# The displaced low part of every eighth k: 192 bytes instead of 160

## The chip, the cores and the metric

The kernel runs on one core of one Trainium2 chip. A core has a matrix engine (TensorE, PE in the profile, with its weight loads as PEld), VectorE (DVE), ScalarE (ACT), GpSimd (POOL) and SyncE (SP), which here issues most of the DMAs. They share an on-chip memory of 128 partitions (SBUF); TensorE writes its sums to a second one (PSUM). The metric is the device time of one execution in microseconds (us), the median of several.

## The reference

The reference is one layer of a decoder over 256 positions with 2048 channels, in float32. Cut to what matters here, it is a row of matrix products with small work between them:

```python
h = rms_norm(x, ln1[l])
proj = h @ w_in[l]                       # GDN q|k|v, beta, decay, gate z; MoBA q|k|v; gates A, B
y_a = gated_deltanet(qkv_a, beta_a, decay_a, z_a, ...) @ w_branch_a[l]
y_b = moba_attention(q_b, k_b, v_b) @ w_branch_b[l]
merged = jax.nn.sigmoid(gate_a) * y_a + jax.nn.sigmoid(gate_b) * y_b
x = x + merged @ w_out[l]
h = rms_norm(x, ln2[l])
u = causal_dwconv(h @ w_up[l], ffn_conv[l], ffn_conv_bias[l])
u_gate, u_val = jnp.split(u, 2, axis=-1)
x = x + (jax.nn.silu(u_gate) * u_val) @ w_down[l]
return rms_norm(x, final_norm)
```

## The kernel before

**Products in two parts.** Every large product is computed from float32 operands that are split in two: a high part in the type `float32r`, and a low part, what is left (`split` and `low`, lines 116 to 121: ACT casts, DVE subtracts). Three matmuls then stand for one: high weight with high operand, high weight with low operand, low weight with high operand. The weights come by DMA in pieces of 1 MB (`fetch`, issued by SP), are split into the tiles `wh` and `wl` (`load_w`), and are the stationary operand, 128 columns at a time. The activations, transposed, are the moving (streamed) operand, 256 columns of 4 bytes, so 1024 bytes in each partition.

**Where the activations lie.** `Parts` (line 152) holds such a split operand in one flat tile. `kt` is the number of 128-row slices of the inner dimension: 16 for 2048 rows, 8 for 1024. For each k the high part lies first and the low part behind it, 1024 bytes each. Eight k make a group (`GROUP`), and each group has 64 elements of room behind it, so that group follows group at 4160 elements. `at(k, a)` gives the place of part `a` (0 high, 1 low) of slice k. In each group the low part of the last k alone (k = 7 and 15) is pushed on by `TURN` elements, into that room; the high parts and all other low parts are not. `one` is a view of one part, `two` of the same part of two neighbouring k. `two` takes the step between the two from `at`, so that it follows the displacement.

Five operands are kept so: `hc` (the first normalized input, 16 k), `yca` and `ycb` (the branches' outputs, 8 k each), `mc` (the merged branches, 16 k) and `h2` (the second normalized input, 16 k, `h` in the profile, in the place of `hc`). They are written by `scaled` (lines 210 and 211) or by `split` and `low`.

**Where the weights lie.** `wh` and `wl` are tiles of 2048 + 64 elements in two buffers each. `chunk` places the weights in them 24 elements (96 bytes) from the start, except for the stages named in `PLACE`: 8 elements for `ps_v`, 16 for `ps_wo`. `load_w` for the last product (`w_dn`) uses the start itself. Weight block follows weight block at 512 bytes.

**The order of the matmuls.** `block` (line 188) runs over k and for each k over the three products: `wh` with the high part, `wh` with the low part, `wl` with the high part. All go through `main_mm` (line 109, its matmul is line 110). `chunk` (line 195) makes two such blocks into one PSUM tile. The stages follow each other as the program is written: `ps_gdn` and `ps_z` (GDN projections; the first two blocks of all use float32 matmuls at line 255 on the raw input), `ps_bd` (line 299: the 16 columns of beta and decay, with the weights `wb2` of 48 columns for each k, its two products through `mmg`), `ps_moba` and `ps_v`, `ps_gate` (16 chunks), `ps_br` (8 chunks for each branch, in turn), `ps_wo` (8 chunks; the first of them in four pieces), `ps_up` (44 chunks), and `pd` (the last product, 512 streamed columns, whose streamed operand is the weights; `Parts` has no share in it). In `ps_v` the operand `hc` is the stationary one.

Beside this stream runs the small work of the two branches (`bg`): `main_mm` counts an estimate of the time that it has issued, and at each 1700 ns lets the generators `gdn`, `moba`, `decay` and `rotary` issue their next piece (`tick`). Their matmuls stand between those of the stages up to the middle of `ps_gate`; behind that nothing of them is left. At the start of `ps_up` two groups of matmuls for the row sums (`rstd`, tile `R`, line 98) stand in the stream, one ahead of it and one within its first block.

Of the kernel before, what the change touches and what calls it, by code (L numbers as in the profile page):

```python
# [27 lines left out]
EPS = 1e-6  # L28
EVERY = 1700
PLACE = {"v": 8, "wo": 16}  # L30
TURN = 40
GROUP = 8
ATT_SCALE = 128 ** -0.5
CONST_FIELDS = [
# [48 lines left out]
def layer_kernel(ctx: ExitStack, tc: tile.TileContext, xT, pos, cst, csel, ceye, vec, convw, ffw, bdv,  # L83
# [68 lines left out]
    class Parts:  # L152
# [6 lines left out]
        def at(self, k, a):  # L159
            return k // GROUP * self.size + (2 * (k % GROUP) + a) * T + TURN * (a and k % GROUP == GROUP - 1)  # L160

# [748 lines left out]
```

## Time and profile before

| | |
|---|---|
| time, median of 3 runs | 1507.69 us (1507.61 to 1507.84) |
| the profiled execution | 1512.56 us |
| its span, first to last instruction | 1510.8 us |
| mean granted TensorE clock | 0.995 |
| TensorE matmuls busy | 1494.0 us, 11471 of them |
| TensorE weight loads busy | 1434.1 us |
| VectorE, ScalarE, GpSimd busy | 968.2, 721.1, 121.1 us |
| HBM read | 271.68 MB, 182 GB/s over the span |

Matmuls are pipelined, and the busy time of a matmul is longer than its distance to the next one, so a share of 99% says that TensorE is never empty, not that it is at its fastest. What counts is the distance from the start of one matmul to the start of the next, and this is read from the timeline. There each row has its start and its length in us, the engine, the line, what it writes and reads, and how many like it in a row are merged (x2). In the page's chain of waits the shares are those of the span.

### The profile page before, as it was taken

The page shows a single profiled execution, that of the slowest core. Times are in us where ns is not written, and L with a number is a line of the kernel's source. Part 1 is how long each engine was busy: PE and PEld are TensorE (multiplying, and loading weights), DVE is VectorE, ACT ScalarE, POOL GpSimd, SP SyncE. Part 2 cuts the span into 40 slices and gives each one's busy share as a digit, 9 for nine tenths or more (in the row PEclk, how much of TensorE's full clock was granted, in tenths as well). Part 3 has the DMA queues.
Part 4 walks back from the last instruction along what each step waited for, and adds up shares of the span by engine and source line. Part 5 has one row for each costly group of instructions (what it writes and reads, how often), then busy time and mean ns, then how long its engine had stood idle before and what let it go on. Part 6 is the DMA issues. An engine that isn't in the chain of part 4 may idle for free.

```text
span 1510.8 us, 26931 instructions
## 1 busy us (share of the span) xinstructions
PE 1494.0 (99%) x11471; PEld 1434.1 (95%) x11471; DVE 968.2 (64%) x1373; ACT 721.1 (48%) x948; POOL 121.1 (8%) x133
## 2 busy tenths in 40 slices
PE   9999999999999999999999999999999999999998
PEld 8999999998999999999999999999999998888886
DVE  7988695886665445666666666666666665555554
ACT  5655363434474433445455444454444554444444
POOL 0001011042120000110100000000000000000000
PEclk9999999999999999999999999999999999999999
DMA  9445444444336553568555555555555554555552
GB/s 341 171 148 184 171 153 162 152 158 144 136 126 209 195 182 125 183 215 303 195 171 195 193 195 187 183 189 196 195 184 184 192 195 167 195 196 195 195 195 84
DMA packets 45657, 277.23 MB, mean 184 GB/s; under 512 B 5504, under 2 KB 6992, under 8 KB 15456
## 3 DMA queue, kind: packets, MB, share of 16 engines
q1 hardware_dynamic: 43712, 270.98, 52.0%
q0 software_dynamic: 960, 2.36, 0.5%
q10 hardware_dynamic: 864, 2.16, 0.4%
q8 instruction: 90, 1.47, 0.4%
q14 instruction: 31, 0.25, 0.0%
HBM read 271.68 MB, written 3.80 MB: 182 GB/s over the span
## 4 chain that ended last, share of the span: by engine, by line
PE 90%; DVE 5%; ACT 2%; DMA 1%; issue 1%; SPq 0%; DVEq 0%; POOLq 0%; ACTq 0%
PE ps_up L110 32%; PE pd L98 16%; PE ps_gate L110 11%; PE ps_gdn L110 8%; PE ps_wo L110 6%; PE ps_br L110 5%; PE ps_moba L110 3%; PE ps_z L110 3%; PE ps_v L110 2%; DVE wl L117 2%; ACT wh L120 1%; DMA wraw<-in_w_gdn 1%; PE g L98 1%; PE py L552 0%; PE pu L558 0%
## 5 line engine op out<-in xcount | busy, mean ns | idle before, releaser
L117 DVE TENSOR_TENSOR wl<-wraw,wh 128x1024 fp32r<-128x1024 f32 (+1 forms) x500 | 607.1, 1248 | 221.6 <-ACT wh L120 221.0
L120 ACT CAST wh<-wraw 128x1024 fp32r<-128x1024 f32 (+1 forms) x500 | 497.5, 1040 | 481.2 <-PE ps_up L110 171.8
L110 PE MATMUL ps_up<-h,wh 128*128 128x256 f32 x2816 | 489.7, 279 | 0.0
L110 PEld LDWEIGHTS ps_up<-h,wh 128*128 128x128 f32 x2816 | 429.4, 189 | 0.1
L110 PE MATMUL ps_up<-h,wl 128*128 128x256 f32 x1408 | 392.4, 279 | 0.0
L110 PEld LDWEIGHTS ps_up<-h,wl 128*128 128x128 f32 x1408 | 264.3, 188 | 0.0
L110 PE MATMUL ps_gate<-hc,wh 128*128 128x256 f32 x1024 | 181.2, 281 | 0.0
L110 PEld LDWEIGHTS ps_gate<-hc,wh 128*128 128x128 f32 x1024 | 157.5, 190 | 0.0
L110 PE MATMUL ps_gate<-hc,wl 128*128 128x256 f32 x512 | 143.5, 281 | 0.2 <-DVE wl L117 0.2
L98 PE MATMUL pd<-wl,ah 128*128 128x512 f32 x336 | 130.8, 389 | 0.0
L98 PE MATMUL pd<-wh,al 128*128 128x512 f32 x336 | 130.8, 389 | 0.0
L110 PE MATMUL ps_gdn<-hc,wh 128*128 128x256 f32 x704 | 126.7, 283 | 0.0
L110 PEld LDWEIGHTS ps_gdn<-hc,wh 128*128 128x128 f32 x704 | 108.9, 191 | 0.9 <-ACT wh L120 0.4
L110 PE MATMUL ps_gdn<-hc,wl 128*128 128x256 f32 x352 | 99.8, 284 | 0.8 <-DVE wl L117 0.8
L110 PEld LDWEIGHTS ps_gate<-hc,wl 128*128 128x128 f32 x512 | 96.8, 189 | 0.4 <-DVE wl L117 0.4
L98 PE MATMUL pd<-wh,ah 128*128 128x512 f32 x336 | 92.8, 391 | 0.0
L110 PE MATMUL ps_moba<-hc,wh 128*128 128x256 f32 x512 | 92.8, 282 | 0.0
L206 DVE TENSOR_TENSOR unf<-ps_up,R 128x512 f32<-128x512 f32 x44 | 30.4, 691 | 95.7 <-PE ps_up L110 95.7
L110 PE MATMUL ps_wo<-mc,wh 128*128 128x256 f32 x512 | 89.2, 279 | 0.0
L110 PEld LDWEIGHTS ps_moba<-hc,wh 128*128 128x128 f32 x512 | 78.5, 189 | 0.2
L110 PEld LDWEIGHTS ps_wo<-mc,wh 128*128 128x128 f32 x512 | 78.1, 189 | 0.0
L98 PEld LDWEIGHTS pd<-wh,al 128*128 128x128 f32 x336 | 63.1, 188 | 13.2
(420 smaller groups left out, 1963.5 us busy)
## 6 DMA issues: line engine op xcount, KB each, us to landing
wraw<-in_w_up SPq DMA_DIRECT2D x88, 1024.0 KB, 4.9
wraw<-in_w_dn SPq DMA_DIRECT2D x44, 1024.0 KB, 4.9
wraw<-in_w_gate SPq DMA_DIRECT2D x32, 1024.0 KB, 4.9
wraw<-in_w_gdn SPq DMA_DIRECT2D x30, 1024.0 KB, 5.0
wraw<-in_w_moba SPq DMA_DIRECT2D x16, 1024.0 KB, 4.9
wraw<-in_w_o SPq DMA_DIRECT2D x16, 1024.0 KB, 5.3
wraw<-in_w_mv SPq DMA_DIRECT2D x8, 1024.0 KB, 5.0
wraw<-in_w_ba SPq DMA_DIRECT2D x16, 512.0 KB, 3.5
```

Source lines behind the costliest of these rows:

```text
L98: pe.matmul(ps, a, b, start=(start and i == 0), stop=(stop and i == n - 1), **kw)
L110: pe.matmul(ps, a, b, start=start, stop=stop, skip_group_check=True)
L117: return (eng or dve).tensor_tensor(lo, src, hi.bitcast(F32), op=ALU.subtract)
L120: act.copy(hi, src)
L206: dve.tensor_tensor(dst, ps, r, op=ALU.mult)
```

## The change

One constant is changed. `TURN` is a number of 4-byte elements; the low part of k = 7 and of k = 15 lies 48 of them, 192 bytes, further on than the regular place, where it lay 40, 160 bytes, further on. The room behind each group is 64 elements before and after, so that no tile changes its size or place and no instruction is added, removed or reshaped.

```diff
 EVERY = 1700
 PLACE = {"v": 8, "wo": 16}
-TURN = 40
+TURN = 48
 GROUP = 8
...
         def at(self, k, a):
             return k // GROUP * self.size + (2 * (k % GROUP) + a) * T + TURN * (a and k % GROUP == GROUP - 1)
```

## The prediction

> **What bounds the kernel now.** I read the page's engine shares and chain of waits first, to see which engine the end hangs on.
>
> ```profile
> span 1510.8 us, 26931 instructions
> PE 1494.0 (99%) x11471; PEld 1434.1 (95%) x11471; DVE 968.2 (64%) x1373; ACT 721.1 (48%) x948; POOL 121.1 (8%) x133
> ...
> PE 90%; DVE 5%; ACT 2%; DMA 1%; issue 1%; SPq 0%; DVEq 0%; POOLq 0%; ACTq 0%
> PE ps_up L110 32%; PE pd L98 16%; PE ps_gate L110 11%; PE ps_gdn L110 8%; PE ps_wo L110 6%; PE ps_br L110 5%; PE ps_moba L110 3%; PE ps_z L110 3%; PE ps_v L110 2%; DVE wl L117 2%; ACT wh L120 1%; DMA wraw<-in_w_gdn 1%; PE g L98 1%; PE py L552 0%; PE pu L558 0%
> ```
>
> TensorE never rests and the chain is 90% TensorE, a third of it in the `ps_up` stage. So the time is a number of matmuls times the distance from one to the next. The change adds and removes no instruction; it can act only through that distance. So I read the timeline of TensorE. In `block` each k is three matmuls: `wh` with the high part, `wh` with the low part, `wl` with the high part. The distance from one `wl` row to the next is one such triplet.
>
> ```profile
> 898.76 0.28 PE L110 MATMUL ps_up<-h,wl 128*128 128x256 f32 x1
> ...
> 900.88 0.28 PE L110 MATMUL ps_up<-h,wl 128*128 128x256 f32 x1
> 901.00 0.40 PE L110 MATMUL ps_up<-h,wh 128*128 128x256 f32 x2
> 901.24 0.28 PE L110 MATMUL ps_up<-h,wl 128*128 128x256 f32 x1
> ...
> 901.58 0.28 PE L110 MATMUL ps_up<-h,wl 128*128 128x256 f32 x1
> ...
> 903.62 0.28 PE L110 MATMUL ps_up<-h,wl 128*128 128x256 f32 x1
> ```
>
> There are two paces. From 898.76 to 900.88 lie 6 triplets in 2.12 us, **353.3 ns** each (slow); from 901.58 to 903.62 6 triplets in 2.04 us, **340.0 ns** (fast). Nothing waits in either. The step between them is the triplet that ends at 901.24, and by its place in the 16 k it is k = 7: the one whose low part lies 160 bytes further on. The same happens at k = 15, back again. So a displaced operand does not cost a fixed amount: it **flips** the stream, and the pace stays until the next flip. Half of all k run slow. Now the stages, by their first and last `wl` rows:
>
> ```profile
> 448.24 0.38 PE L110 MATMUL ps_gate<-hc,wl 128*128 128x256 f32 x1 [0.22 <-DVE wl L117]
> ...
> 448.70 0.28 PE L110 MATMUL ps_gate<-hc,wl 128*128 128x256 f32 x1
> ...
> 450.40 0.28 PE L110 MATMUL ps_gate<-hc,wl 128*128 128x256 f32 x1
> ...
> 587.12 0.28 PE L110 MATMUL ps_gate<-hc,wl 128*128 128x256 f32 x1
> ```
> ```profile
> 679.31 0.28 PE L110 MATMUL ps_br<-ycb,wl 128*128 128x256 f32 x1
> ...
> 679.65 0.28 PE L110 MATMUL ps_br<-ycb,wl 128*128 128x256 f32 x1
> ...
> 680.01 0.28 PE L110 MATMUL ps_wo<-mc,wl 128*128 128x256 f32 x1
> ...
> 683.19 0.28 PE L110 MATMUL ps_wo<-mc,wl 128*128 128x256 f32 x1
> ...
> 768.80 0.28 PE L110 MATMUL ps_wo<-mc,wl 128*128 128x256 f32 x1
> ```
> ```profile
> 776.09 0.28 PE L110 MATMUL ps_up<-h,wl 128*128 128x256 f32 x1
> ...
> 1259.81 0.28 PE L110 MATMUL ps_up<-h,wl 128*128 128x256 f32 x1
> ```
>
> `ps_up`: from k = 15 of its first block to k = 15 of its 88th lie 87 x 16 = 1392 triplets in 483.72 us, 347.5 ns each. Half fast and half slow would be 346.7; the rest, 0.8 ns, is what the flips themselves cost. `ps_wo`: 255 triplets in 88.79 us, 348.2 each. `ps_gate` from 448.70 on: 398 triplets in 138.42 us, 347.8 each.
>
> **The change, part by part.** Only one address moves: the low part of k = 7 and 15 goes from +160 to +192 bytes. All other steps between operands of a stream are whole multiples of 64 bytes: 1024 from part to part, 256 extra from group to group, 512 from one weight block to the next, 8448 from `wh` to `wl`. None of these flips the pace; 160 = 2.5 x 64 does. 192 = 3 x 64 belongs with those that don't. The nearest row for a step of just 192 bytes is the `ps_bd` product, whose weights `wb2` have 48 columns and so advance by 192 bytes at each k (two matmuls):
>
> ```profile
> 33.20 3.84 PE L98 MATMUL ps_bd<-hc,wb 128*48 128x256 f32 x32
> ...
> 34.78 2.25 PE L98 MATMUL ps_bd<-hc,wb 128*48 128x256 f32 x18
> 36.88 1.03 PE L98 MATMUL R<-sq,ones 128*128 128x256 f32 x4
> ```
>
> The first row is the whole product (32 matmuls from 33.20), the second what is left of it from 34.78 on (18). The first 14, which take seven steps of 192 bytes in the weights, need 1.58 us, 112.9 ns each: the fast pace, undisturbed. The other 18, behind the displaced k = 7, need 2.10 us, 116.7 each. So I take it that **192 bytes don't flip**, and each stretch keeps the pace with which it starts. It is the weights that step there, not the streamed operand, so a chance is left for the opposite.
>
> What becomes of each stage then is decided by what starts it. *`ps_gate` from 448.70*: behind the wait for `wl` it runs fast at once, 448.70 to 450.40 is 5 triplets in 1.70 us. Kept, 398 x 340.0 = 135.3 us: **-3.1**. *`ps_br`*: 8 chunks x 2 x 2 blocks x 8 k = 256 triplets, of which each block of 8 is now fast or slow in turn; it inherits the fast pace, and behind each of its waits for `wl` the fast one comes too:
>
> ```profile
> 671.59 0.39 PE L110 MATMUL ps_br<-yca,wl 128*128 128x256 f32 x1 [0.24 <-DVE wl L117]
> ...
> 672.39 0.28 PE L110 MATMUL ps_br<-yca,wl 128*128 128x256 f32 x1
> ...
> 674.09 0.28 PE L110 MATMUL ps_br<-yca,wl 128*128 128x256 f32 x1
> ```
>
> (5 triplets in 1.70 us.) So 128 x 13.3 ns are saved: **-1.7**. The waits stay, and a faster TensorE may lengthen them by as much, which would make it 0. *`ps_wo`*: its weights lie at 16 elements instead of 24, a step of 32 bytes, half of 64 as 160 is. It starts slow (680.01 to 683.19, 9 triplets in 3.18 us), but there a flip at the last k of `ps_br` and that step come together. I take the step alone as one flip, fast to slow: 255 x 353.3 = 90.1 us, **+1.3**; if it does nothing, 86.7 us, -2.1. *`ps_up`*: its start is broken twice by the row sums (`R`), once ahead of it and once behind k = 13:
>
> ```profile
> 770.01 0.28 PE L110 MATMUL ps_up<-h,wl 128*128 128x256 f32 x1
> ...
> 772.39 0.28 PE L110 MATMUL ps_up<-h,wl 128*128 128x256 f32 x1
> ```
> ```profile
> 774.52 0.28 PE L110 MATMUL ps_up<-h,wl 128*128 128x256 f32 x1
> 774.64 1.02 PE L98 MATMUL R<-sq,ones 128*128 128x256 f32 x4
> 775.31 0.59 PE L110 MATMUL ps_up<-h,wh 128*128 128x256 f32 x2
> 775.74 0.28 PE L110 MATMUL ps_up<-h,wl 128*128 128x256 f32 x1
> ...
> 778.57 0.28 PE L110 MATMUL ps_up<-h,wl 128*128 128x256 f32 x1
> ```
>
> Behind the first break it ran fast (7 triplets in 2.38 us from 770.01), behind the second slow: 775.74 to 778.57 is 8 triplets in 2.83 us, 353.8 each. After that second break nothing interrupts the stage again, so this restart sets the pace of all 1392 triplets: slow, 491.8 us, **+8.1**; fast, 473.3 us, **-10.4**. I take slow, the row of this very restart; moreover the stream that entered it was slow, and with `ps_wo` slow it would be again. *The stages before 448* are cut into short pieces by the other branches' work:
>
> ```profile
> L110 PE MATMUL ps_gdn<-hc,wh 128*128 128x256 f32 x704 | 126.7, 283 | 0.0
> ...
> L110 PE MATMUL ps_moba<-hc,wh 128*128 128x256 f32 x512 | 92.8, 282 | 0.0
> ...
> L110 PE MATMUL ps_z<-hc,wh 128*128 128x256 f32 x256 | 45.6, 280 | 0.0
> ```
>
> Two `wh` to a triplet: 736 triplets, and the 113 of `ps_gate` ahead of 448.70, 849. All slow would be +5.6, all fast -5.6 (half of them x 13.3 ns); restarts go both ways, and I take 0. *Writing* the displaced part costs what it did, since shapes and counts are the same; DVE is 64% busy and stands beside TensorE, so that a few ns there would be hidden.
>
> Sum: -3.1 - 1.7 + 1.3 + 8.1 + 0 = **+4.6 us**. The profiled execution took 1512.56 us, its span 1510.8 and 1.8 around it; it would take 1517.2. The runs shown have a median of 1507.69, 4.9 under the profiled one, so the profile's paces may not all be theirs; I carry the difference over: 1512.3.
>
> **The rivals.** *The frozen pace of `ps_up` is fast* (the other side: faster). Mechanism and place are the restart behind the second `R`; it decides from whether the first triplets behind it come at 340 or 353. For it: the restart at 770.01, behind the same kind of `R`, is fast, and a stage entered differently (no flip just ahead) may restart differently. Against it: the row at 775.74. Price: -10.4 - 3.1 - 1.7 + 1.3 = -13.9, **1493.8**; with `ps_wo` fast too 1490.4.
>
> *192 bytes flip as 160 do, or the place doesn't matter at all*: **1507.7**. For it: the flip was seen with one displacement of the streamed operand alone. Against it: `ps_bd`.
>
> The Trainium skill, "TensorE: Matmul & The Clock Gate", section "Step-by-step: what each phase is for", says that PE has two independent SBUF read ports, so that loading the next weights takes nothing from the running matmul. By that rule an operand's place could not set the pace, and the change would give 1507.7. The two paces of one form of matmul in the rows above, with the step at the displaced k, speak against it.
>
> **How the numbers follow.** A measurement of this kernel can tell about 0.2%, 3.0 us, from no change. Frozen with `ps_up` slow: 0.42, predicted 1512.3, its own range 1507 to 1516 (stages before 448 at half their bounds, `ps_wo` either way). Frozen with `ps_up` fast: 0.36, 1490 to 1497. No difference: 0.22. A part of the first case, 0.04, ends within 0.2% (`ps_wo` fast), and a part of the third, 0.01 on either side, outside it: slower 0.39, within 0.24, faster 0.37. Two cases of both signs hold most of the chance, so the range runs over both, 1490 to 1516.
>
> **What would show it.** In the changed kernel's timeline no triplet changes its pace at k = 7 or 15; if pace still changes there, the third case holds. The triplets of `ps_up` lie 353 apart throughout (or 340: then 1494). `ps_gate` behind 448 and `ps_br` at 340, `ps_wo` at 353. I would be wrong altogether if a third pace appeared, or if frozen streams drifted from slow to fast without a flip, as the second half of `ps_bd` may (116.7 is below the slow 117.8): then faster.

## The result and the profile after

| | before | after |
|---|---|---|
| time, median of 4 runs of each on one chip | 1507.76 us (1507.61 to 1510.16) | **1497.61 us** (1495.45 to 1498.88) |
| the profiled execution | 1512.56 us | 1497.02 us |
| its span | 1510.8 us | 1495.2 us |

The ratio is 0.9927, with a 95% interval of 0.991 to 0.9945: the changed kernel is 10 us faster. Predicted were 1512.3 us, 4.6 us slower. Of the runs further down, four of the eight of e1 lie over 1.5% above its fastest and count as slow, at the same granted clock as its others (0.997 to 0.999 in all eight). The page of the changed kernel, its span, engines and chain of waits:

```profile
span 1495.2 us, 26931 instructions
PE 1476.9 (99%) x11471; PEld 1416.5 (95%) x11471; DVE 967.7 (65%) x1373; ACT 720.8 (48%) x948; POOL 121.2 (8%) x133
...
PE 92%; DVE 4%; ACT 1%; DMA 1%; issue 1%; SPq 0%; DVEq 0%; ACTq 0%
```

The counts are those of before on every engine, and TensorE is as full as it was. So it is the distance between matmuls that shrank. Where it shrank is seen from the starts of the stages. These are groups of the two kernels (columns: count, shortest/median/longest duration in ns, first to last start in us), before and then after; `identb` is the first row of the last product:

```profile
L110 PE MATMUL ps_gate<-hc,wh x1024: 276/281/562, 394.1 to 587.0; 128*128 128x256 f32 x171
L110 PE MATMUL ps_br<-yca,wh x256: 276/280/286, 587.2 to 674.0; 128*128 128x256 f32 x128
L110 PE MATMUL ps_wo<-mc,wh x512: 275/281/286, 679.8 to 768.7; 128*128 128x256 f32 x171
L110 PE MATMUL ps_up<-h,wh x2816: 276/280/467, 769.6 to 1259.7; 128*128 128x256 f32 x188
L795 PE MATMUL pd<-identb,x x32: 270/272/273, 1259.9 to 1268.2; 128*128 128x128 f32 x32
```
```profile
L110 PE MATMUL ps_gate<-hc,wh x1024: 276/276/561, 389.9 to 580.6; 128*128 128x256 f32 x171
L110 PE MATMUL ps_br<-yca,wh x256: 276/276/288, 580.8 to 666.9; 128*128 128x256 f32 x128
L110 PE MATMUL ps_wo<-mc,wh x512: 276/276/285, 672.6 to 760.1; 128*128 128x256 f32 x171
L110 PE MATMUL ps_up<-h,wh x2816: 276/276/470, 761.0 to 1244.2; 128*128 128x256 f32 x188
L795 PE MATMUL pd<-identb,x x32: 270/272/273, 1244.4 to 1252.7; 128*128 128x128 f32 x32
```

From one first start to the next: `ps_gate` 193.1 us before and 190.9 after (-2.2), `ps_br` 92.6 and 91.8 (-0.8), `ps_wo` 89.8 and 88.4 (-1.4), `ps_up` 490.3 and 483.4 (-6.9). Another 4.2 us are gained ahead of `ps_gate`, and none behind `ps_up`: the last product starts 15.5 us earlier, which is the whole difference of the two spans (15.6).

Not all of it belongs to the change. The windows view (columns: length, busy TensorE with the matmuls that begin, granted clock, DMA share, GB/s), first of before and then of after, shows a throttled stretch that of these two profiles only the one of before has:

```profile
75.00:100.00 25.00, 25.00 (x178) 0.86 0.43 144
```
```profile
75.00:100.00 25.00, 25.00 (x206) 1.00 0.46 154
```

There 28 matmuls fewer began at a granted clock of 0.86; at 117 ns each these are 3.3 us. Without them the two profiles differ by 12.2 us, and the medians by 10.15. The rest is the spread of the runs: the profiled execution of before, less 3.3, still lies 1.5 above the median of those runs, and that of after lies 0.6 below its own.

Now the timeline of `ps_up` after, by the rows of `wl`, one to a triplet. First its beginning, with the second break by the row sums:

```profile
763.55 0.28 PE L110 MATMUL ps_up<-h,wl 128*128 128x256 f32 x1
763.90 0.28 PE L110 MATMUL ps_up<-h,wl 128*128 128x256 f32 x1
764.26 0.28 PE L110 MATMUL ps_up<-h,wl 128*128 128x256 f32 x1
764.60 0.28 PE L110 MATMUL ps_up<-h,wl 128*128 128x256 f32 x1
...
765.96 0.28 PE L110 MATMUL ps_up<-h,wl 128*128 128x256 f32 x1
766.07 1.02 PE L98 MATMUL R<-sq,ones 128*128 128x256 f32 x4
...
767.17 0.28 PE L110 MATMUL ps_up<-h,wl 128*128 128x256 f32 x1
767.53 0.28 PE L110 MATMUL ps_up<-h,wl 128*128 128x256 f32 x1
767.88 0.28 PE L110 MATMUL ps_up<-h,wl 128*128 128x256 f32 x1
768.22 0.28 PE L110 MATMUL ps_up<-h,wl 128*128 128x256 f32 x1
...
1244.29 0.28 PE L110 MATMUL ps_up<-h,wl 128*128 128x256 f32 x1
```

The stream enters slow. The row at 763.90 is that of k = 7; the next step is still 0.36, and from 764.26 on the steps are 0.34. So the displaced k = 7 turned a slow stream fast: 192 bytes act. Behind the break the first step is 0.36 again (767.17 to 767.53), and 767.53 is k = 15, itself displaced; one step of 0.35 follows, and then 0.34. Whether this restart was slow can't be read from two triplets, the second of them displaced. The steps from matmul to matmul there, in ns, worked out from the traces (from the second matmul of k = 14 on; behind the bar the low part of k = 15 has begun), say more:

```
before, 160 bytes:  117 118 118 | 120 118 117 119 117 118   slow up to k = 7
e1, none displaced: 117 118 119 | 117 117 119 117 118 117   stays slow
after, 192 bytes:   120 116 116 | 123 118 117 116 114 113   fast
e12, none displaced:120 117 115 | 115 113 113 114 113 113   fast
```

Ahead of the bar the changed kernel goes as e12 does, which came out fast with nothing displaced (e1 and e12 are described below), and not as the two streams that stayed slow. So this restart was probably fast by itself. What 192 bytes do to a fast stream is seen later (1005.91 is k = 7):

```profile
1004.88 0.28 PE L110 MATMUL ps_up<-h,wl 128*128 128x256 f32 x1
1005.22 0.28 PE L110 MATMUL ps_up<-h,wl 128*128 128x256 f32 x1
1005.56 0.28 PE L110 MATMUL ps_up<-h,wl 128*128 128x256 f32 x1
1005.91 0.28 PE L110 MATMUL ps_up<-h,wl 128*128 128x256 f32 x1
1006.26 0.28 PE L110 MATMUL ps_up<-h,wl 128*128 128x256 f32 x1
1006.60 0.28 PE L110 MATMUL ps_up<-h,wl 128*128 128x256 f32 x1
```

0.34, 0.34, 0.35, 0.35, 0.34: a short slow patch, and then fast as before it. From 767.53 to 1244.29 lie the same 1392 triplets as in the prediction, in 476.76 us, 342.5 ns each. All fast they would take 473.3; the 3.5 us more, over 87 x 2 displaced k, are **20 ns for each displaced k**. The displaced k is also seen to turn slow into fast in two stretches of `ps_gate`, at 412.9 and 427.2 us. So the stretches are fast without a flip, at a small price.

### The profile page after: what moved, and what is told of

Same layout as the page of the kernel before. It is cut to its first block, busy times and chain, and to the rows that moved or that the text cites. A ratio compares the mean times of both kernels' runs of the same rounds, so it can differ in the third digit from the quotient of the medians.

```text
span 1495.2 us, 26931 instructions
## 1 busy us (share of the span) xinstructions
PE 1476.9 (99%) x11471; PEld 1416.5 (95%) x11471; DVE 967.7 (65%) x1373; ACT 720.8 (48%) x948; POOL 121.2 (8%) x133
## 4 chain that ended last, share of the span: by engine, by line
PE 92%; DVE 4%; ACT 1%; DMA 1%; issue 1%; SPq 0%; DVEq 0%; ACTq 0%
PE ps_up L110 32%; PE pd L98 16%; PE ps_gate L110 11%; PE ps_gdn L110 8%; PE ps_wo L110 6%; PE ps_br L110 5%; PE ps_moba L110 4%; PE ps_v L110 3%; PE ps_z L110 3%; DVE wl L117 2%; DMA wraw<-in_w_gdn 1%; ACT wh L120 1%; PE g L98 1%; PE py L552 1%; PE pu L558 1%
## 5 line engine op out<-in xcount | busy, mean ns | idle before, releaser
L110 PE MATMUL ps_up<-h,wh 128*128 128x256 f32 x2816 | 482.8, 277 | 0.0
L110 PEld LDWEIGHTS ps_up<-h,wh 128*128 128x128 f32 x2816 | 425.1, 188 | 0.1
L110 PE MATMUL ps_moba<-hc,wh 128*128 128x256 f32 x512 | 92.6, 282 | 0.0
```

The costliest lines, as they stand in the source:

```text
L110: pe.matmul(ps, a, b, start=start, stop=stop, skip_group_check=True)
```

## The experiments

The question was by what rule a displaced k acts on the pace, and whether that explains the gain. Two positions of the prediction were on trial: that a stream keeps its pace unless something acts on it and finds a new one at each restart, and that whole multiples of 64 bytes do nothing. The expectations below name their theories as they were put on record before each run. As one measure for all kernels I take the first to the last start of the `wh` rows of `ps_up`, as in the groups above: 490.1 us before, 483.2 after.

### Other distances

All of these change one number. This is e1; e2 has 16 elements, e3 32, e4 64, e7 56, e8 24, and e16, which came last, 8:

```diff
-TURN = 48
+TURN = 0
```

> No part is displaced (0 bytes). Theory A (a displaced read nudges the stream; without a nudge each stretch keeps the pace with which it starts): no triplet changes its pace at k = 7 or 15, and each stage runs wholly at 340 or wholly at 353 ns; ps_up decides, 1392 x 340 = 473 or x 353 = 492 us, the whole near 1490 or near 1511 us. Theory B (the stream finds the fast pace by itself and every displacement only costs): 340 ns in all stages, ps_up 473 us, the whole near 1490, some 8 us (396 displaced k x 20 ns) below the changed kernel.

> Displaced by 64 bytes, 1 x 64. Theory A1 (whole multiples of 64 act alike): as with 192, one slow patch of some 20 ns at each k = 7 and 15 and 340 ns between, ps_up near 483 us, the whole near 1497. Theory A2 (the size counts, each its own way): another pattern, either no patch at all, as with no displacement, or a flip that stays, as with 160, with ps_up near 490.

> Displaced by 128 bytes, 2 x 64. Theory A1 (whole multiples of 64 act alike): as with 192, a patch of some 20 ns at each displaced k, ps_up near 483 us, the whole near 1497. Theory A2 (the size counts): another pattern, ps_up between 473 and 492.

> Displaced by 256 bytes, the step that also lies between the two groups, where no pace changes. Theory A1 (whole multiples of 64 act alike): ps_up near 483 us as with 192. Theory A2 (the place within some longer period counts, and 256 is a whole one): nothing at k = 7 and 15, and each stage as it is with no displacement, to within 1 us of that run in ps_up.

> Displaced by 224 bytes, the nearest place above 192. Theory A2 (256 bytes are one round, and the nudge grows or shrinks over it): between 192 (ends fast) and 256 (nothing): ends fast, with a patch of under 20 ns, ps_up 476 to 483 us. Theory E (an odd multiple of 32 flips, an even one does not): flips as 160 does, ps_up near 490.

> Displaced by 96 bytes, between 64 (mostly ends fast) and 128 (ends slow). Theory A2 (one round of 256): between the two, ps_up 484 to 498 us. Theory E (an odd multiple of 32 flips): half the k slow, ps_up near 490 us and 347.5 ns a triplet.

> TURN 8 (32 bytes), the last of the steps of 32 bytes that has not been run. If what counts is how far the displaced part is from a whole round of 256 bytes, to either side, 32 acts as 224 does: ends fast, ps_up about 481.6 us. If the side counts, as 96 (ends fast) and 160 (flips) suggest, which are equally far from 256: it does something else, flips (ps_up 489 us), ends slow (498) or nothing.

| displaced by | run | time, us | `ps_up`, us | what a displaced k does |
|---|---|---|---|---|
| 0 | e1 | 1515.38, median of 8 (1492.86 to 1523.16) | 498.3 | nothing |
| 32 bytes | e16 | 1501.52 | 483.2 | leaves a fast stream fast, for 20 ns; leaves a slow stretch slow |
| 64 | e2 | 1498.17 | 484.4 | leaves a fast stream fast, for 27 ns; turns some slow stretches |
| 96 | e8 | 1497.71 | 483.2 | leaves a fast stream fast, for 20 ns; turns some slow stretches |
| 128 | e3 | 1522.69 | 498.1 | ends slow, with few exceptions |
| 160 | before | 1507.76 | 490.1 | flips |
| 192 | after | 1497.61 | 483.2 | leaves a fast stream fast, for 20 ns; turns nearly all slow stretches |
| 224 | e7 | 1494.16 | 482.1 | leaves a fast stream fast, for 13 ns; turns about half of the slow stretches |
| 256 | e4 | 1515.15 | 498.3 | nothing |

The rows of before and after are the medians of the result; e1 ran eight times, the others once. They ran on three chips, on which before took 1508.8 to 1510.4 us. The rows of e1 in `ps_up`, its group and the `wl` rows behind the second break and at the end, show a stream on which nothing acts:

```profile
L110 PE MATMUL ps_up<-h,wh x2816: 280/281/469, 767.4 to 1265.7; 128*128 128x256 f32 x188
```
```profile
773.59 0.28 PE L110 MATMUL ps_up<-h,wl 128*128 128x256 f32 x1
773.94 0.28 PE L110 MATMUL ps_up<-h,wl 128*128 128x256 f32 x1
...
1265.78 0.28 PE L110 MATMUL ps_up<-h,wl 128*128 128x256 f32 x1
```

Slow behind the break (0.35), and from 773.94 to 1265.78 the 1392 triplets take 491.84 us, 353.3 ns each to the end. The shortest of the 2816 matmuls lasts 280 ns and the median one 281: not one of them is of the fast kind, whose median above is 276. So a stream does keep its pace. 256 bytes do as little as none, 64 and 128 both act, in opposite ways: it is a **round of 256 bytes** in which the place counts, not one of 64.

A fast `ps_up` does not yet say that the displaced k made it fast. Between the two breaks, with 32, 64, 96 and 224 bytes, the stream came slow to k = 7 and stayed slow; behind the second break it ran fast. These are the `wl` rows of e14 (224 bytes, described below) from k = 7 on, 0.35 to 0.36 apart:

```profile
762.41 0.28 PE L110 MATMUL ps_up<-h,wl 128*128 128x256 f32 x1
762.76 0.28 PE L110 MATMUL ps_up<-h,wl 128*128 128x256 f32 x1
763.11 0.28 PE L110 MATMUL ps_up<-h,wl 128*128 128x256 f32 x1
763.47 0.28 PE L110 MATMUL ps_up<-h,wl 128*128 128x256 f32 x1
```

So I counted, from `ps_gate` on, the displaced k that met a slow stream and had three whole triplets on either side. With 192 bytes 6 of 6 turned it fast (after and e13), with 224 it was 13 of 23 (e7 and e14), with 64 5 of 9, with 96 2 of 6, with 32 none of 12; with 0 and 256 bytes none of the places did, in over 200 each. Of the places tried 192 bytes alone brought every slow stretch of these stages to the fast pace. It isn't without exception: in `ps_moba`, which is cut up by other work, two slow stretches stayed slow at a displaced k in each of the two runs. Within the round the effect follows no simple distance: 96 and 160 are equally far from 256, and the one leaves a fast stream fast where the other flips it. Why a slow stretch turns at some displaced k and not at others is left open.

### Only one operand

`h2` alone, the operand of `ps_up`, is displaced by 192 bytes, all others by 160 as before:

```diff
-            return k // GROUP * self.size + (2 * (k % GROUP) + a) * T + TURN * (a and k % GROUP == GROUP - 1)
+            return k // GROUP * self.size + (2 * (k % GROUP) + a) * T + self.turn * (a and k % GROUP == GROUP - 1)
...
-    h2 = Parts(hp, KD, "h2", tag="hc")
+    h2 = Parts(hp, KD, "h2", turn=48, tag="hc")
```

> One part alone: 192 bytes in h2 (the stage ps_up) and 160 in the four other operands. Theory A (each displaced read acts on the stream that reads it): ps_up near 342.6 ns a triplet and 482.7 us as in the changed kernel, the stages before near 348 as in the kernel before, the whole 7 us under the kernel before. Theory C (the gain comes from elsewhere, the clock or the waits of the early stages): ps_up stays near 347.5 and 489.7 us, the whole within 2 us of the kernel before.

1502.66 us beside 1510.38 for before on that chip; `ps_up` 483.1 us, as in the changed kernel, and the stages ahead of it at their old paces. So the operand of a stage acts on that stage, and 7.0 us of the gain are made by `h2`.

### The weights' side

In e6 nothing is displaced in the streamed operands. Instead the weights of `ps_up` lie at 8 elements in place of 24, and the weights of k = 15 are pushed 48 elements (192 bytes) further on:

```diff
-TURN = 48
+TURN = 0
...
+            o = k * P + (48 if k == KD - 1 and wh.shape[1] > 2048 else 0)
...
-                main_mm(ps[:, j], w_[:, k, :], x.one(k, a), j == k == a == 0 and w_ is wh,
+                main_mm(ps[:, j], w_[:, o:o + P], x.one(k, a), j == k == a == 0 and w_ is wh,
...
-                ws[j] = load_w(blocks[j], kt * P, raw=raws[j], piece=piece, at=PLACE.get(name, 24))
+                ws[j] = load_w(blocks[j], kt * P, raw=raws[j], piece=piece, at=8, push=48) if name == "up" else load_w(
+                    blocks[j], kt * P, raw=raws[j], piece=piece, at=PLACE.get(name, 24))
```

> No part of the streamed operands is displaced; in ps_up the weights start at 8 elements instead of 24 and those of k = 15 lie 192 bytes further on, in wh and wl. Theory A3 (the place of the streamed operand alone nudges): no triplet of ps_up changes its pace at k = 15, all at 340 or all at 353. Theory D (the place of the weights relative to the stream nudges just as well): a slow patch or a change of pace at each k = 15, ps_up between 476 and 492 us with a period of 48 matmuls.

1520.51 us, `ps_up` 505.9. The timeline shows a third pace, and what the push does to it:

```profile
1000.08 0.28 PE L110 MATMUL ps_up<-h,wl 128*128 128x256 f32 x1
...
1002.96 0.28 PE L110 MATMUL ps_up<-h,wl 128*128 128x256 f32 x1
...
1009.06 0.28 PE L110 MATMUL ps_up<-h,wl 128*128 128x256 f32 x1
1009.40 0.28 PE L110 MATMUL ps_up<-h,wl 128*128 128x256 f32 x1
```

Eight triplets in 2.88 us are 360 ns each. The triplet of the pushed weights is the one that ends at 1009.40. From the start of each of its three matmuls to the next start it is 113, 113 and 114 ns (worked out from the trace), where the others take 120. So the place of the weights acts too. I take it that the place of the operand relative to its weights is what counts; no run moved both alike, so this is not shown.

If so, another relation with nothing displaced might be fast in itself. In e9, e10 and e11 all weights of the products with `hc`, `yca`, `ycb`, `mc` and `h2` (but for `ps_v`) lie further on. This is e9; e10 has 40 and, for `ps_wo`, 32, and e11 has 32 and 24:

```diff
-PLACE = {"v": 8, "wo": 16}
-TURN = 48
+PLACE = {"v": 8, "wo": 48}
+TURN = 0
...
-                ws[j] = load_w(blocks[j], kt * P, raw=raws[j], piece=piece, at=PLACE.get(name, 24))
+                ws[j] = load_w(blocks[j], kt * P, raw=raws[j], piece=piece, at=PLACE.get(name, 56))
```

> Nothing is displaced (TURN 0); instead all weights of the products with hc, yc, mc and h2 lie 128 bytes further on (place 56 instead of 24, ps_wo 48 instead of 16), so that the streamed operand starts 64 bytes after its weights, counted in rounds of 256 bytes; so far it was 192. Theory 'the distance between the operand and its weights, modulo 256 bytes, sets the pace': the weights of k = 15 lay at just this distance in e6 and ran at 113 ns, so all triplets of ps_up, ps_wo, ps_br and ps_gate come at 340 ns: ps_up 479 us, whole about 1490 us. Rival 'without a displacement the pace is frozen at a restart, at any distance': ps_up is 479 or 498 us whole, by chance, and stages differ from one another as in e1.

> As e9, with the weights at 40 (ps_wo 32): the streamed operand starts 128 bytes after its weights, modulo 256. Theory of the distance: one pace in all stages, the same after every restart; which one is not known from the runs so far, 340 (ps_up 479 us) or between 353 and 360 (498 to 506 us). Rival: frozen by chance at 340 or 353, differing from stage to stage.

> As e9, with the weights at 32 (ps_wo 24): the streamed operand starts 160 bytes after its weights, modulo 256, halfway between the whole multiples of 64. Theory of the distance: one pace in all stages, 340 to 360 ns a triplet, unlike e9 or e10 by more than 3 us in ps_up. Rival, the pace is frozen by chance: 340 or 353 from stage to stage.

The groups of e9, e10 and e11 in turn:

```profile
L110 PE MATMUL ps_up<-h,wh x2816: 279/279/467, 773.2 to 1271.5; 128*128 128x256 f32 x188
```
```profile
L110 PE MATMUL ps_up<-h,wh x2816: 281/284/469, 777.3 to 1285.0; 128*128 128x256 f32 x188
```
```profile
L110 PE MATMUL ps_up<-h,wh x2816: 277/280/468, 773.6 to 1270.0; 128*128 128x256 f32 x188
```

e9 took 1524.38 us with `ps_up` at 498.3: 340 at this relation was a wrong guess. The weights of k = 15 in e6 lay at the same 8 + 48 = 56 elements and ran fast, and here a stream started slow and stayed so. In e9 itself the first three blocks of `ps_wo` ran at 340, up to a break, and the rest at 353. So the relation allows both paces, as the old one does, and the rival (frozen by chance) held. e10 took 1537.81 us, `ps_up` 507.7: every triplet of `ps_up` takes 360 ns, the slowest of all and neither pace of the rival, though other stages of e10 ran otherwise. e11 took 1522.86 us, `ps_up` 496.4, 352 ns a triplet. No place tried is fast by itself.

### The row that misled

The prediction took from `ps_bd` that steps of 192 bytes do nothing. In e12 the same product loads 128 weight columns at the same steps, in place of 48; the added columns' results are not used:

```diff
-    mmg(s, [(wb2[:, k, :], hc.one(k, a)) for k in range(KD) for a in range(2)])
+    mmg(s, [(wbf[:, 48 * k:48 * k + P], hc.one(k, a)) for k in range(KD) for a in range(2)])
```

> Nothing is displaced (TURN 0), and ps_bd loads 128 weight columns for each k in place of 48, at the same steps of 192 bytes (the 80 added columns are those of the next k, and their rows of the result are not used). It tests the row from which the prediction took that 192 bytes do nothing. Theory 'the row was blind, since a load of 48 columns takes 121 ns and one of 128 columns 188': now the distance between operand and weights goes through four values in turn, and the pace within ps_bd follows with a period of 4 k (8 matmuls), a quarter of them at about 120 ns. Rival 'steps of the weights by 192 bytes do nothing, only the streamed operand's do': all 32 matmuls at one pace, 113 or 118 ns, as with 48 columns. The whole: 1493 to 1523 us as e1, since nothing is displaced.

The weight loads of e1, where the product has its 48 columns, and of e12:

```profile
L98 PEld LDWEIGHTS ps_bd<-hc,wb x32: 119/121/125, 33.1 to 36.7; 128*48 128x48 f32 x32
```
```profile
L98 PEld LDWEIGHTS ps_bd<-hc,wb x32: 187/188/192, 33.1 to 36.7; 128*128 128x128 f32 x32
```

And the 32 distances from start to start in ns, worked out from the two traces, eight to a line:

```
e1,   48 columns: 118 120 117 117 117 120 116 118
                  113 116 115 119 116 115 116 119
                  117 117 116 119 116 117 118 117
                  115 118 120 117 113 118 118 116
e12, 128 columns: 113 118 113 117 118 120 120 121
                  113 118 113 117 118 120 120 121
                  113 118 113 117 118 120 120 121
                  113 118 113 117 118 120 120 122
```

Eight matmuls are four k, and four steps of 192 bytes are three rounds of 256. With loads of 128 columns the pace follows the place, in strict repetition; with loads of 48 columns, which take 121 ns in place of 188, it shows no period. So the row was blind to what it was asked.

### Keeping the fast pace without the price

If a stream keeps its pace, one displaced k now and then may be enough. In e15 `mc` and `h2` are not displaced, and a displaced copy of the low part of k = 15 stands in for it in one block of every 4th chunk of `ps_wo` and every 8th of `ps_up`; the other operands are displaced by 224 bytes. It ran beside the changed kernel (e13) and the one with 224 bytes (e14, `TURN = 56`):

```diff
-    mc = Parts(m, KD, "mc")
+    mc = Parts(m, KD, "mc", turn=0)
+    mk = m.tile([P, 320], F32R, name="mk")[:, 56:56 + T]
...
-        ps = chunk([w_up[c], w_up[NF + c]], h2, KD, "up")
+        ps = chunk([w_up[c], w_up[NF + c]], h2, KD, "up", kick=hk if c % 8 == 0 else None)
...
-                main_mm(ps[:, j], w_[:, k, :], x.one(k, a), j == k == a == 0 and w_ is wh,
+                main_mm(ps[:, j], w_[:, k, :], kick if kick is not None and j == 0 and a and k == kt - 1 else x.one(k, a), j == k == a == 0 and w_ is wh,
```

> The changed kernel once more, unaltered, as the measure for e14 and e15 on the same chip: 1497 to 1499 us, ratio to before 0.991 to 0.9945.

> TURN 56 (224 bytes), timed. If what is left in the changed kernel is the price of each displaced k (about 20 ns at 192 bytes, 12 at 224), the some 750 displaced k of the long stages give 6 us less at most and 2 to 4 us likely: 1494 to 1496, ratio 0.989 to 0.992. Rival: the 1494.16 of e7 was a run with lucky restarts; then no different from e13.

> The displaced low part is used only to bring the stream to the fast pace, not at every group: mc and h2 are not displaced, and a displaced copy (224 bytes) of the low part of k = 15 stands in for it in one block of every 4th chunk of ps_wo and every 8th of ps_up (2 and 6 times); hc, yca and ycb are displaced by 224 bytes as in e14. If a stream keeps its pace unless something acts on it, ps_up comes at 340 to 341 ns a triplet, 479 to 480 us (e14: 481.6), and the whole is 2 to 3 us below e14: 1491 to 1493. Rivals: a single displaced k does not always bring the fast pace, so that some stretches of 16 blocks stay slow, each of them costing 16 x 16 x 13.3 ns = 3.4 us: 1495 to 1500, unlike from run to run; or the copies cost time ahead of ps_wo and ps_up, where TensorE waits: the same as e14.

| | median, us | range of the runs | ratio to before (95%) | `ps_up`, us |
|---|---|---|---|---|
| before | 1508.81 | 1507.38 to 1511.6 (9) | | |
| e13, 192 bytes | 1496.07 | 1495.06 to 1497.13 (4) | 0.9912 (0.9899 to 0.9926) | 483.2 |
| e14, 224 bytes | 1496.01 | 1494.16 to 1499.04 (5) | 0.9915 (0.9899 to 0.993) | 482.1 |
| e15 | **1493.41** | 1493.01 to 1496.2 (4) | 0.9898 (0.9885 to 0.9912) | 479.6 |

The timeline of e15 shows the first use of the copy in `ps_wo` (`mk`), and then the same 1392 triplets of `ps_up` as above by their ends:

```profile
680.37 0.28 PE L110 MATMUL ps_wo<-mc,wl 128*128 128x256 f32 x1
...
680.73 0.28 PE L110 MATMUL ps_wo<-mc,wl 128*128 128x256 f32 x1
680.84 0.28 PE L110 MATMUL ps_wo<-mc,wh 128*128 128x256 f32 x1
680.96 0.28 PE L110 MATMUL ps_wo<-mk,wh 128*128 128x256 f32 x1
681.08 0.29 PE L110 MATMUL ps_wo<-mc,wl 128*128 128x256 f32 x1
...
681.43 0.28 PE L110 MATMUL ps_wo<-mc,wl 128*128 128x256 f32 x1
...
681.77 0.28 PE L110 MATMUL ps_wo<-mc,wl 128*128 128x256 f32 x1
```
```profile
767.18 0.28 PE L110 MATMUL ps_up<-h,wl 128*128 128x256 f32 x1
...
1240.54 0.28 PE L110 MATMUL ps_up<-h,wl 128*128 128x256 f32 x1
```

`ps_wo` came slow (0.36, and 0.35 with the copy in it), has one more step of 0.35, and then goes on at 0.34 to its end, with one patch at the second copy: a single displaced matmul turned it. `ps_up` takes 473.36 us, 340.06 ns a triplet, and has six copies among its 4224 matmuls. But it was fast ahead of the first of them, and e12 ran this stage as fast with none (479.6 us). So here the copies did no harm; that they held the pace is not shown by this profile. It is 3.4 us less in `ps_up` than in the changed kernel, and the median is 2.7 us lower; the intervals of the two ratios still overlap, so that it is the stage, not the whole, that shows the gain beyond doubt. The four runs of e15 lie within 3.2 us, those of e1 within 30; this speaks for the displaced parts of e15, the copies and the others together. The 224 bytes of e14 do save 1.1 us in `ps_up`, but the whole shows no difference from e13, and the 1494.16 of e7 was at the low end of the runs with 224 bytes.

## Why the prediction was wrong

- **A number of matmuls times a distance** (held). The counts are equal and the chain is TensorE's; writing the displaced part cost nothing that shows (DVE 968.2 before, 967.7 after).
- **192 bytes don't flip** (the step that failed). As it was put, all other steps of a stream are whole multiples of 64 bytes, none of them acts, and 192 belongs with them, the nearest row being that of `ps_bd`. But the steps named there, 1024, 256, 512 and 8448 bytes, are all whole multiples of 256 too; they could not tell a round of 64 from one of 256. And the row of `ps_bd` was taken from loads of another width, of which e12 shows that they hide the effect. 192 bytes do not flip, true, but they do not leave the pace alone: from `ps_gate` on a slow stream turned fast at all 6 displaced k that met one, and a fast one stays fast for 20 ns each. The prediction asked that no triplet change its pace at k = 7 or 15; the rows at 763.90 and 764.26 show one that does. Stage by stage the terms were -3.1 (`ps_gate`), -1.7 (`ps_br`), +1.3 (`ps_wo`) and +8.1 (`ps_up`); the stages moved by -2.2, -0.8, -1.4 and -6.9. In the first two mainly the price of the displaced k is missing; the last two have the wrong sign.
- **Each stretch keeps the pace with which it starts** (held where nothing acts, e1 and e4; here something does). The forecast of the frozen stages came out well there: `ps_up` slow with 491.8 us for its 1392 triplets, 491.84 in e1. The single run with 256 bytes gave 1515.15 us and the median of e1 was 1515.38, against the predicted 1512.3. It came out for another displacement, and with some luck: the restart was slow in these two profiles and fast in e12.
- **Which pace a restart gives** was read from one row, and should have been called a chance. Of the eight triplets of that row seven lie behind the displaced k = 15, where by the prediction's own rule the pace flips, so that they could not tell the pace of the restart. It was slow, as the steps 117, 118, 118 above show, and there k = 15 did not flip it. e1 ran between 1492.86 and 1523.16 us with one program. Only one of these runs has a profile, but e12, which differs from it in `ps_bd` alone, had `ps_up` fast from end to end (479.6 us), where e1 and e4 had it slow; with `ps_gate` it was the other way, slow in e12 behind its last wait and fast in e1.
- **The rival "`ps_up` is fast"**, 1493.8 us, was nearest, and half its road was right. It reckoned with a restart that may go otherwise when entered otherwise, and the steps behind the second break look like such a fast restart. But the pace was not frozen: each of the 174 displaced k disturbs it, so that the 1392 triplets took 476.76 us and not 473.3. Nor was it luck alone: the slow stream ahead of the break was turned at k = 7, and a slow restart would have met the next displaced k, which turned such a stream in 6 of 6 cases from `ps_gate` on. What part the restart had in this run stays open.
- **The rival "flips as 160 does or the place doesn't matter"** fell with the timeline: paces still change at the displaced k, but not as a flip, and the time is not 1507.7.
- **The profile's own excess over the median** (4.9 us carried over) was real: 3.3 us of it is the throttled window between 75 and 100 us.

The Trainium skill, "TensorE: Matmul & The Clock Gate", section "Step-by-step: what each phase is for", gives PE two independent SBUF read ports, by which loading weights takes nothing from the running matmul. That a place cannot set the pace, as the prediction had it "by that rule", goes further than this sentence. The runs show that the place of the weights does set it for these matmuls: in e6 it is 113 ns with the pushed weights and 120 with the others, the operand unmoved. What in the chip has a round of 256 bytes, and why 160 flips where 192 ends fast, no run here shows.

## What to carry to other kernels

Where one form of matmul shows two distances with nothing waiting, look at where the streamed operand and the weights lie, counted in rounds of 256 bytes, and try the displacements on the chip: here they span 1494 to 1523 us and no rule foretold them. When a stage comes out fast, look whether the displacement turned it or whether it started fast. A rule read off from "these steps do nothing" is only as good as the steps are different; ask which other rule the same rows would bear. And a stream with nothing displaced is not safe, since its pace is found anew at restarts; 192 bytes turned every slow stretch from `ps_gate` on, and the rare copies of e15 gave the lowest median.

## What the runs showed of the hardware

- The matmuls of one form (128 x 128 weights, 256 streamed columns of 4 bytes) follow each other in `ps_up` at 113.3, 117.3, 117.8 or 120 ns in the mean (340, 352, 353.3 and 360 a triplet), with the granted clock at 0.997 to 0.999 in the runs that show them. Which one depends on where operand and weights lie (a step of 256 bytes changes nothing, smaller ones do), and for some places on the past of the stream.
- A stream with nothing displaced held such a pace over 4176 matmuls, slow in e1 and fast in e12. One displaced matmul was enough to change it, by 192 bytes at k = 7 of `ps_up` (after) and by 224 bytes in `ps_wo` (e15).
- A displaced k that leaves a fast stream fast costs 13 ns at 224 bytes, 20 at 32, 96 and 192, and 27 at 64.
- One program without a displaced part ran in 1492.86 to 1523.16 us, eight times on one chip, its lower four in 1492.86 to 1514.84; the programs with 192 bytes kept within 1495.06 to 1498.88 in eight runs.
